# Five groups of projection columns instead of six, and one run of NSA's value products for both tiles, in a two-layer mLSTM, MoBA and NSA trunk

## The chip, the cores and the metric

The kernel runs on one core of a Trainium2 chip. The metric is the device time of one execution in microseconds; the median of the runs counts. All inputs lie in the chip's memory (HBM) when it starts, and the output is written back there. The core has TensorE (matmuls, called PE in the profile, its weight loads PEld), VectorE (DVE), ScalarE (ACT), GpSimd (POOL) and SyncE (SP, which here only issues DMAs).

## The reference

Two layers over 256 tokens of width 1024. Each layer projects the normalised input once, into 3476 columns that feed three kinds of heads, and then runs a feed-forward part:

```
for l in range(2):
    h = rmsnorm(x, norm_mix[l])
    proj = h @ w_in[l]                       # 1024 x 3476
    (m_q, m_k, m_v, m_o,                     # 512 each: mLSTM
     m_i, m_f,                               # 4 each: mLSTM's gates
     b_q, b_k, b_v,                          # 256 each: MoBA
     n_q, n_kc, n_vc,                        # 256, 64, 64: NSA, queries and compressed branch
     n_ks, n_vs, n_kw, n_vw, n_g             # 64 each and 12: NSA, selected and window branch, gates
    ) = split(proj)
    y = concat(mlstm(...), moba(...), nsa(...))
    x = x + y @ w_out[l]
    h = rmsnorm(x, norm_ffn[l])
    x = x + square(relu(h @ w_ff1[l])) @ w_ff2[l]
```

At this length MoBA is causal attention over all 256 tokens with 4 heads of 64. NSA has 4 query heads of 64 that share one key and value head per branch. Its selected branch and its window branch both become causal attention over all tokens (branches 1 and 2 in the code), its compressed branch (branch 0) attends to 15 compressed positions, and three gates per head weigh the branches.

## The kernel before, in words

The 256 tokens are two tiles of 128, `i` = 0 and 1. Every float32 product is made of three passes of a rounded type: high part times high part, high times low, low times high. Weights come from HBM in pieces into `raw` (five buffers); ACT casts a piece into its high part `hi`, DVE subtracts to get `lo` (six buffers of each). The input's parts are `H`, the mixed heads' are `Mh` and `Ml`.

The columns of the projection are cut into groups. `ORDER` (line 30) gives the order in a layer, `GROUPS` (line 378) their first column and width:

```
ORDER = ("o1", "o6", "o2", "o3", "c0", "c1", "q0", "c2", "c3", "o4", "q1", "q2", "q3", "o5")
GROUPS = {"o1": (C_NQ, 384), "o2": (C_KS, 268), "o3": (C_G, 264), "o4": (C_BK, 512), "o5": (C_MV, 512), "o6": (C_MO, 512)}
```

o1 holds NSA's queries and the inputs of its compressed branch; o2 NSA's keys and values of branches 1 and 2 and its gates; o3 mLSTM's gates and MoBA's queries; o4 MoBA's keys and values; o5 and o6 mLSTM's values and output gates. Such a group is 48 matmuls a layer in `project`: two tiles, eight blocks of 128 rows, three passes, with a block of the input as the stationary operand and the group's columns moving. Each tile's sum is one PSUM bank (tag `acc`, two of them). q0 to q3 are mLSTM's queries and keys in transposed form, c0 to c3 the weights of NSA's compression. The rest of PSUM is six banks of the tag `wk`.

The order of the work on every engine is written out by a planner (class `Flow`) while the program is built. Each part of the work is a generator that yields its operations; the planner estimates when each is ready and what it costs, and takes the next by readiness and rank. The projection, the output projection and the feed-forward part form one generator (`main`, rank 100) that fills TensorE whenever no smaller operation is ready. The casts and subtractions come up when a piece is due within a set time. A generator that asks for a buffer of a tag waits until one has been freed.

The small work that the change touches:

- `cmp_inputs` copies o1's queries into `R` (two buffers) and the compressed inputs into `KV`.
- `nsa_heads` copies o2's keys into `R`, the values into `VS`, the gates into `GT`, normalises (the power of the mean square runs on POOL, tile `hr`), rotates and transposes into `QK`.
- `gates` reads o3: mLSTM's gates into `GI`, MoBA's queries into two new `R` buffers (`R2`). `moba_heads` adds o4's keys to them, normalises and frees them.
- `score` makes the masked exponentials of NSA's scores per tile (`P`, three buffers). `attention` then runs, per tile, `attend` for branches 1 and 2: scale `P` by gate over sum, transpose it in blocks (`ident` times `P`), copy the blocks to `PT` (four buffers), and multiply with `VS` in one burst, 8 matmuls in tile 0 and 16 in tile 1, each with 64 stationary columns. The sum stays in a `wk` bank, one for each tile, until `cmp_attend` adds branch 0 (`PcT` times `VC`) and the result is split into `Mh` and `Ml`.
- `numerators` puts mLSTM's output tiles into `Y` (two buffers of 512 columns).
- `out_project` starts with NSA's and MoBA's rows and ends with mLSTM's.

Of the kernel before, what the change touches and what calls it, by code (L numbers as in the profile page):

```python
# [11 lines left out]
ALU = mybir.AluOpType  # L12
# [16 lines left out]

ORDER = ("o1", "o6", "o2", "o3", "c0", "c1", "q0", "c2", "c3", "o4", "q1", "q2", "q3", "o5")  # L30

# [251 lines left out]
def body(ctx, tc, x, w_in, b_if, conv_qk, m_norm, moba_g, nsa_qg, nsa_kg, cmp_pe, cmp_w1, cmp_w2,  # L283
# [91 lines left out]
    def rows(w, k0, kk, c0, n):  # L375
        return [(w[k0 * 128:(k0 + kk) * 128, c0:c0 + n].rearrange("(k p) n -> p k n", p=128), None)], kk, n

    GROUPS = {"o1": (C_NQ, 384), "o2": (C_KS, 268), "o3": (C_G, 264), "o4": (C_BK, 512), "o5": (C_MV, 512),
              "o6": (C_MO, 512)}
    WO_ORDER = [6, 7, 4, 5, 0, 1, 2, 3]  # L380
# [13 lines left out]
    for l in range(DEPTH):  # L394
        for name in ORDER:
            if name[0] == "c":
                s = int(name[1])
                pieces.append(([(cmp_w1[l, a, s * 512:(s + 1) * 512, :].rearrange("(k p) n -> p k n", p=128), a)
                                for a in range(2)], 8, 128))
                due.append(t)  # L400
                t += 0.45
            elif name[0] == "q":
                pieces += [rows(w_in[l], 4 * s, 4, int(name[1]) * 256, 256) for s in range(2)]
                due += [t, t + 12 * 288 / 2400]
                t += 48 * 288 / 2400
            else:
                n = GROUPS[name][1]
                pieces += [rows(w_in[l], 2 * s, 2, *GROUPS[name]) for s in range(4)]
                due += [t + 6 * s * (n + 32) / 2400 for s in range(4)]
                t += 48 * (n + 32) / 2400  # L410
# [13 lines left out]

    whole = {j for j, p in enumerate(pieces) if len(p[0]) == 2}
    raws, parts = {}, {}
# [3 lines left out]
    def loads(unsplit):  # L430

        for j, (srcs, kk, n) in enumerate(pieces):
# [8 lines left out]
            for src, a in srcs:  # L441
                dst = raw[:, :kk * n] if a is None else raw[:, a * 512:(a + 1) * 512]
                yield sy.dma_start(dst.rearrange("p (k n) -> p k n", n=n), src)
            done.add(f"raw {j}")
# [76 lines left out]
    class Layer:  # L521
        def __init__(self):
# [3 lines left out]
            for name, shape, dt in (("H", (8, 2, S), F32R), ("Mh", (8, S), F32R),  # L526
# [4 lines left out]
                setattr(self, name, keep(name, *shape, dt=dt))  # L531
            self.GT = [keep(f"GT{i}", 12) for i in range(2)]

            self.Hh, self.Hl = (self.H[:, :, a, :] for a in range(2))
            self.Fh, self.Fl = self.Hh, self.Hl

    Ls = [Layer() for _ in range(DEPTH)]
# [255 lines left out]
    def first_smalls():  # L793
        yield "H017"
        yield from small_loads(0, 0)
        yield gp.tensor_copy(B[:, 0:128], ident)
        yield gp.tensor_copy(B[:, 128:416], C[:, K_NM - 128:K_NM + 160])
        per = yield new("dg", 128)
        yield sy.dma_start(per[:64], cmp_pe.rearrange("l a (i j) d -> (l a i) (j d)", j=2))
        pps = yield wk()  # L800
        yield tr(pps[:, :64], per[:64], ident[:64, :64])
        yield dv.tensor_copy(PEs, pps[:, :64].rearrange("p (l a i) -> p l a i", l=2, a=2))
# [96 lines left out]
    def cmp_inputs(l):  # L899
# [3 lines left out]
        for i in range(2):  # L903
# [6 lines left out]
            L.R.append((yield new("R", 8, 64)))  # L910
            yield act(L.R[i][:, 0:4].rearrange("p a d -> p (a d)"), o[:, 0:256], AF.Copy, scale=L.rs[i])
            free(o)
            done.add(f"R{l}{i}")
# [20 lines left out]
    def nsa_heads(l, i):  # L934
# [4 lines left out]
        o, R, GT = L.o["o2"][i], L.R[i], L.GT[i]  # L939
        kv = o[:, 0:256].rearrange("p (a b d) -> p a b d", a=2, b=2)  # L940
        yield act(R[:, 4:6], kv[:, :, 0, :], AF.Copy, scale=L.rs[i])
        yield act(L.VS[:, i], kv[:, :, 1, :], AF.Copy, scale=L.rs[i])

        yield ts(GT, o[:, 256:268], L.rs[i], 0.5, op0=ALU.mult, op1=ALU.mult)
        free(o)
        N = yield new("N", 10, 64)
# [56 lines left out]
    def gates(l):  # L1003
# [5 lines left out]
        for i in range(2):  # L1009
            yield f"o3{l}{i}"  # L1010
            yield f"rs{l}{i}"
            o = L.o["o3"][i]
            yield stt(GI[:, i], o[:, 0:8], L.rs[i], BIFs[:, l], op0=ALU.mult, op1=ALU.add)
            L.R2.append((yield new("R", 8, 64)))
            yield act(L.R2[i][:, 0:4].rearrange("p a d -> p (a d)"), o[:, 8:264], AF.Copy, scale=L.rs[i])
            free(o)
            done.add(f"bq{l}{i}")
# [103 lines left out]

    def attend(i, P, sm, gates, o, values, last):

        nk = (i + 1) * 128
        n = len(P)
        yield dv.reciprocal(sm, sm)
        T = []
        for b in range(n):
            yield tt(sm[:, b], sm[:, b], gates[b].rearrange("p (a b) -> p b a", b=2), op=ALU.mult)
# [11 lines left out]
        ops = []  # L1141
        for b in range(n):
            for s in range(i + 1):
                for p in range(2):
                    for h in range(2):
                        ops.append(mm(o[64 * h:64 * h + 64, p, :], values(b, s, 2 * p + h),
                                      T[b * (i + 1) + s][:, 2 * p + h, :], start=b + s + p == 0,
                                      stop=last and b == n - 1 and s == i, skip_group_check=True))
        yield Burst(ops)
        free(*T)  # L1150

# [105 lines left out]

    def attention(l, units):
        L = Ls[l]
        for i, brs in units:  # L1260
            yield f"s{l}{i}{brs}"
            P, sm = L.held.pop((i, brs))
            if brs != (0,):
                o = yield wk(2, 128)
            if brs == (0,):
                yield from cmp_attend(L, i, P, sm, o)
            else:
                yield from attend(i, P, sm, [L.GT[i][:, br * 4:br * 4 + 4] for br in brs], o,
                                  lambda b, s, h: L.VS[:, s, brs[b] - 1, :], False)
            if brs == (0,):  # L1270
                yield from split(L.Mh[:, 6:8, tokens(i)], L.Ml[:, 6:8, tokens(i)], o)
                free(o)
                done.add(f"nsa{l}{i}")

# [123 lines left out]
    for l in range(DEPTH):  # L1398
        gens = [after_mix(l, i, n) for i, n in tiles] + [after_ffn(l, i, n) for i, n in tiles]
        gens += [square_scales(l), scales(l), cmp_inputs(l)]  # L1400
        gens += [nsa_heads(l, i) for i in range(2)] + [cmp_keys(l), gates(l)] + [moba_heads(l, i) for i in range(2)]
        gens += [attention(l, nsa), score(l, nsa), values(l), out_gates(l)] + [numerators(l, i) for i in range(2)]
        gens += [mlstm(l)] + [conv(l, c) for c in range(4)] + [moba_attend(l), moba_scores(l)]
# [38 lines left out]
```

## Time and profile before

| | |
|---|---|
| median of 3 runs | 639.02 us (638.28 to 639.03) |
| the profiled execution | 639.09 us, span 637.3 us from first to last instruction |
| mean granted TensorE clock | 0.999 |
| PE busy | 629.8 us, 3799 matmuls |
| DVE, ACT, POOL busy | 443.3, 366.6, 30.0 us |
| read from HBM | 111.06 MB |

A matmul record is one pass of a matmul; a float32 product that is not split by hand appears as two records. A busy time adds up what ran at any moment. The records of consecutive matmuls overlap, so the time that one costs in a dense stretch is the distance from its start to the next one's start. A row of the timeline gives the start, the length, the engine, the line (that of a helper here, the same for all), the operation, the tiles written and read, the stationary and moving sizes and how many records were merged.

### The profile page before, as it was taken

The page shows a single profiled execution, that of the slowest core. Times are in us where ns is not written, and L with a number is a line of the kernel's source. Part 1 is how long each engine was busy: PE and PEld are TensorE (multiplying, and loading weights), DVE is VectorE, ACT ScalarE, POOL GpSimd, SP SyncE. Part 2 cuts the span into 40 slices and gives each one's busy share as a digit, 9 for nine tenths or more (in the row PEclk, how much of TensorE's full clock was granted, in tenths as well). Part 3 has the DMA queues.
Part 4 walks back from the last instruction along what each step waited for, and adds up shares of the span by engine and source line. Part 5 has one row for each costly group of instructions (what it writes and reads, how often), then busy time and mean ns, then how long its engine had stood idle before and what let it go on. Part 6 is the DMA issues. An engine that isn't in the chain of part 4 may idle for free.

```text
span 637.3 us, 10219 instructions
## 1 busy us (share of the span) xinstructions
PE 629.8 (99%) x3799; PEld 544.1 (85%) x3799; DVE 443.3 (70%) x823; ACT 366.6 (58%) x718; POOL 30.0 (5%) x50
## 2 busy tenths in 40 slices
PE   9999999999999999999999999999999999999997
PEld 8898898888888888888899879988888888888885
DVE  6778899678574656656594879987776565665661
ACT  7679685655464535444465886845645554545440
POOL 1010200100000000000010111001000000000000
PEclk9999999999999999999999999999999999999999
DMA  8896524349565565646456924254466556564601
GB/s 310 238 304 210 156 67 140 124 137 284 170 203 194 182 211 160 216 163 200 125 153 212 301 69 142 69 167 152 154 212 212 184 187 209 167 214 156 222 34 67
DMA packets 79378, 112.78 MB, mean 177 GB/s; under 512 B 4928, under 2 KB 61792, under 8 KB 79328
## 3 DMA queue, kind: packets, MB, share of 16 engines
q1 hardware_dynamic: 79152, 112.05, 55.5%
q8 instruction: 30, 0.49, 0.3%
q14 instruction: 20, 0.16, 0.1%
q10 hardware_dynamic: 176, 0.07, 0.0%
HBM read 111.06 MB, written 1.05 MB: 176 GB/s over the span
## 4 chain that ended last, share of the span: by engine, by line
PE 91%; DMA 3%; ACT 2%; DVE 2%; issue 1%; POOL 1%; SPq 0%; ACTq 0%; DVEq 0%; POOLq 0%
PE wk L137 57%; PE acc L137 35%; DMA raw<-in_w_in 2%; ACT hi L137 1%; DVE lo L137 1%; DMA ident<-in_cst 1%; POOL hr L137 0%; SPq L136 0%; DVE N L137 0%; ACT QK L137 0%; POOL rs L137 0%; DVE dg L137 0%; ACT R L137 0%; DVE x L137 0%; DVE hss L137 0%
## 5 line engine op out<-in xcount | busy, mean ns | idle before, releaser
L137 DVE TENSOR_TENSOR lo<-raw,hi 128x1024 fp32r<-128x1024 f32 (+4 forms) x209 | 240.4, 1167 | 123.3 <-ACT hi L137 122.6
L137 ACT CAST hi<-raw 128x1024 fp32r<-128x1024 f32 (+3 forms) x207 | 205.9, 1015 | 135.0 <-PE wk L137 111.7
L137 PE MATMUL wk<-H,hi 128*128 128x512 f32 x512 | 128.0, 391 | 0.0
L137 PEld LDWEIGHTS wk<-H,hi 128*128 128x128 f32 x512 | 93.7, 188 | 17.9
L137 PE MATMUL acc<-hi,H 128*128 128x512 f32 (+3 forms) x368 | 99.2, 351 | 0.0
L137 PE MATMUL acc<-hi,P 128*128 128x512 f32 x240 | 79.3, 391 | 0.2 <-DVE P L137 0.2
L137 PE MATMUL wk<-hi,P 128*128 128x512 f32 x240 | 78.8, 389 | 0.0
L137 PEld LDWEIGHTS wk<-H,lo 128*128 128x128 f32 x512 | 69.9, 190 | 5.0
L137 PE MATMUL wk<-H,lo 128*128 128x256 f32 x512 | 71.4, 282 | 0.0
L137 PEld LDWEIGHTS acc<-hi,H 128*128 128x128 f32 x368 | 64.0, 188 | 6.5 <-issue 0.4
L137 PE MATMUL acc<-lo,H 128*128 128x512 f32 (+3 forms) x184 | 65.3, 355 | 0.0
L137 PEld LDWEIGHTS acc<-hi,P 128*128 128x128 f32 x240 | 45.1, 188 | 9.4 <-DVE P L137 0.6
L137 PEld LDWEIGHTS wk<-hi,P 128*128 128x128 f32 x240 | 45.0, 188 | 9.4
L137 PE MATMUL acc<-H,hi 128*128 128x256 f32 x256 | 51.5, 292 | 0.0
L137 PE MATMUL acc<-lo,P 128*128 128x512 f32 x120 | 47.0, 392 | 0.0
L137 PE MATMUL wk<-lo,P 128*128 128x512 f32 x120 | 46.7, 389 | 0.0
L137 ACT COPY th<-wk 128x256 f32<-128x256 f32 x64 | 23.9, 373 | 35.7 <-PE wk L137 35.7
L137 PEld LDWEIGHTS acc<-H,hi 128*128 128x128 f32 x256 | 40.7, 190 | 0.5 <-ACT hi L137 0.2
L137 PEld LDWEIGHTS acc<-lo,H 128*128 128x128 f32 x184 | 34.6, 188 | 3.4 <-issue 0.3
L137 PE MATMUL acc<-H,lo 128*128 128x256 f32 x128 | 36.7, 287 | 0.0
L137 ACT ACTIVATE H<-wk,V 128x128 fp32r<-128x128 f32 x64 | 18.1, 375 | 21.1 <-PE wk L137 21.1
L137 ACT CAST P<-cv 128x512 fp32r<-128x512 f32 x30 | 18.6, 621 | 17.3 <-DVE cv L137 17.3
(199 smaller groups left out, 799.5 us busy)
## 6 DMA issues: line engine op xcount, KB each, us to landing
raw<-in_w_ff SPq DMA_DIRECT2D x128, 512.0 KB, 4.4
raw<-in_w_in SPq DMA_DIRECT2D x40, 512.0 KB, 5.0
raw<-in_w_out SPq DMA_DIRECT2D x16, 512.0 KB, 4.0
whole<-in_cmp_w SPq DMA_DIRECT2D x16, 256.0 KB, 5.0
raw<-in_w_in SPq DMA_DIRECT2D x8, 384.0 KB, 3.9
raw<-in_w_in SPq DMA_DIRECT2D x8, 268.0 KB, 3.5
raw<-in_w_in SPq DMA_DIRECT2D x8, 264.0 KB, 3.2
out<-x SPq DMA_DIRECT2D x4, 256.0 KB, 2.0
```

Of the source, the lines that this page charges most:

```text
L137: o = Op(self.name, lambda: f(out, *args, **kw), outs, ins, self.cost(op, outs, ins))
```

## The change

It does four things. The three groups o1, o2 and o3 become two: o1 takes the KS columns behind its own (448 columns), and o2 takes the rest of the old o2 and all of the old o3 (468 columns, loaded by two DMAs to a piece). A bank of o2 is freed when both of its readers, `nsa_heads` and `gates`, have read it. MoBA's queries (`R2`) go into the two `Y` buffers instead of `R`. NSA's `attention` becomes `nsa_attend`: the weights of both tiles are scaled and transposed first, those of tile 0 into the two `Y` buffers and those of tile 1 into `PT`; then all 24 value products run as one burst into one `wk` bank, and then the compressed branch is added for both tiles. Besides, the small load of `cmp_pe` goes into a `Y` buffer and is issued ahead of the other small loads.

```diff
-ORDER = ("o1", "o6", "o2", "o3", "c0", "c1", "q0", "c2", "c3", "o4", "q1", "q2", "q3", "o5")
+ORDER = ("o1", "o6", "o2", "c0", "c1", "q0", "c2", "c3", "o4", "q1", "q2", "q3", "o5")
...
-    GROUPS = {"o1": (C_NQ, 384), "o2": (C_KS, 268), "o3": (C_G, 264), "o4": (C_BK, 512), "o5": (C_MV, 512),
-              "o6": (C_MO, 512)}
+    GROUPS = {"o1": (C_NQ, 448), "o2": (C_KS + 64, 468), "o4": (C_BK, 512), "o5": (C_MV, 512), "o6": (C_MO, 512)}
...
-                pieces += [rows(w_in[l], 2 * s, 2, *GROUPS[name]) for s in range(4)]
+                if name == "o2":
+                    pieces += [([(w_in[l, 256 * s:256 * s + 256, c0:c0 + m].rearrange("(k p) n -> p k n", p=128),
+                                      slice(at, at + m)) for c0, m, at in ((C_KS + 64, 204, 0), (C_G, 264, 204))], 2, n)
+                                   for s in range(4)]
+                else:
+                    pieces += [rows(w_in[l], 2 * s, 2, *GROUPS[name]) for s in range(4)]
...
+            self.left = [2, 2]
+        def read(self, i):
+            self.left[i] -= 1
+            if not self.left[i]:
+                free(self.o["o2"][i])
...
         yield "H017"
+        per = yield new("Y", 512)
+        yield sy.dma_start(per[:64, :128], cmp_pe.rearrange("l a (i j) d -> (l a i) (j d)", j=2))
         yield from small_loads(0, 0)
...
-        per = yield new("dg", 128)
-        yield sy.dma_start(per[:64], cmp_pe.rearrange("l a (i j) d -> (l a i) (j d)", j=2))
...
+            yield act(L.R[i][:, 4], o[:, 384:448], AF.Copy, scale=L.rs[i])
             free(o)
...
-        yield act(R[:, 4:6], kv[:, :, 0, :], AF.Copy, scale=L.rs[i])
-        yield act(L.VS[:, i], kv[:, :, 1, :], AF.Copy, scale=L.rs[i])
-        yield ts(GT, o[:, 256:268], L.rs[i], 0.5, op0=ALU.mult, op1=ALU.mult)
-        free(o)
+        yield act(R[:, 5], o[:, 64:128], AF.Copy, scale=L.rs[i])
+        yield act(L.VS[:, i], o[:, 0:256].rearrange("p (a b) -> p a b", a=2)[:, :, 0:64], AF.Copy, scale=L.rs[i])
+        yield ts(GT, o[:, 192:204], L.rs[i], 0.5, op0=ALU.mult, op1=ALU.mult)
+        L.read(i)
...
-            o = L.o["o3"][i]
-            yield stt(GI[:, i], o[:, 0:8], L.rs[i], BIFs[:, l], op0=ALU.mult, op1=ALU.add)
-            L.R2.append((yield new("R", 8, 64)))
-            yield act(L.R2[i][:, 0:4].rearrange("p a d -> p (a d)"), o[:, 8:264], AF.Copy, scale=L.rs[i])
-            free(o)
+            o = L.o["o2"][i]
+            yield stt(GI[:, i], o[:, 204:212], L.rs[i], BIFs[:, l], op0=ALU.mult, op1=ALU.add)
+            L.R2.append((yield new("Y", 8, 64)))
+            yield act(L.R2[i][:, 0:4].rearrange("p a d -> p (a d)"), o[:, 212:468], AF.Copy, scale=L.rs[i])
+            L.read(i)
...
-                T.append((yield new("PT", 4, 128)))
-                yield copy(T[-1], pt)
+                T.append((b, s, (yield new("PT" if i else "Y", 4, 128))))
+                yield copy(T[-1][2], pt)
...
+    def nsa_attend(l, brs):
+        L = Ls[l]
+        T = []
+        for i in range(2):
+            yield f"s{l}{i}{brs}"
+            P, sm = L.held.pop((i, brs))
+            T.append((yield from weighted(i, P, sm, [L.GT[i][:, br * 4:br * 4 + 4] for br in brs])))
+        o = yield wk(2, 2, 128)
+        yield Burst([mm(o[64 * h:64 * h + 64, i, p, :], L.VS[:, s, brs[b] - 1, :], t[:, 2 * p + h, :],
+                        start=i + b + s + p == 0, stop=False, skip_group_check=True)
+                     for i in range(2) for b, s, t in T[i] for p in range(2) for h in range(2)])
+        free(*(t for u in T for *_, t in u))
+        for i in range(2):
+            yield f"s{l}{i}{(0,)}"
+            yield from cmp_attend(L, i, *L.held.pop((i, (0,))), o[:, i])
+            yield from split(L.Mh[:, 6:8, tokens(i)], L.Ml[:, 6:8, tokens(i)], o[:, i])
+            done.add(f"nsa{l}{i}")
+        free(o)
```

More of the change, by code (lines that the diff above doesn't have):

```diff
@@ L423, in body @@
                 t += 12 * 544 / 2400
-    whole = {j for j, p in enumerate(pieces) if len(p[0]) == 2}
+    whole = {j for j, p in enumerate(pieces) if p[1] == 8}
     raws, parts = {}, {}
@@ L441, in loads @@
             for src, a in srcs:
-                dst = raw[:, :kk * n] if a is None else raw[:, a * 512:(a + 1) * 512]
-                yield sy.dma_start(dst.rearrange("p (k n) -> p k n", n=n), src)
+                dst = raw[:, a * 512:(a + 1) * 512] if j in whole else raw[:, :kk * n]
+                dst = dst.rearrange("p (k n) -> p k n", n=n)
+                yield sy.dma_start(dst[:, :, a] if isinstance(a, slice) else dst, src)
             done.add(f"raw {j}")
@@ L797, in first_smalls @@
         yield gp.tensor_copy(B[:, 128:416], C[:, K_NM - 128:K_NM + 160])
-        per = yield new("dg", 128)
-        yield sy.dma_start(per[:64], cmp_pe.rearrange("l a (i j) d -> (l a i) (j d)", j=2))
         pps = yield wk()
-        yield tr(pps[:, :64], per[:64], ident[:64, :64])
+        yield tr(pps[:, :64], per[:64, :128], ident[:64, :64])
         yield dv.tensor_copy(PEs, pps[:, :64].rearrange("p (l a i) -> p l a i", l=2, a=2))
@@ L939, in nsa_heads @@
         o, R, GT = L.o["o2"][i], L.R[i], L.GT[i]
-        kv = o[:, 0:256].rearrange("p (a b d) -> p a b d", a=2, b=2)
-        yield act(R[:, 4:6], kv[:, :, 0, :], AF.Copy, scale=L.rs[i])
-        yield act(L.VS[:, i], kv[:, :, 1, :], AF.Copy, scale=L.rs[i])
-        yield ts(GT, o[:, 256:268], L.rs[i], 0.5, op0=ALU.mult, op1=ALU.mult)
-        free(o)
+        yield act(R[:, 5], o[:, 64:128], AF.Copy, scale=L.rs[i])
+        yield act(L.VS[:, i], o[:, 0:256].rearrange("p (a b) -> p a b", a=2)[:, :, 0:64], AF.Copy, scale=L.rs[i])
+        yield ts(GT, o[:, 192:204], L.rs[i], 0.5, op0=ALU.mult, op1=ALU.mult)
+        L.read(i)
         N = yield new("N", 10, 64)
@@ L1009, in gates @@
         for i in range(2):
-            yield f"o3{l}{i}"
+            yield f"o2{l}{i}"
             yield f"rs{l}{i}"
-            o = L.o["o3"][i]
-            yield stt(GI[:, i], o[:, 0:8], L.rs[i], BIFs[:, l], op0=ALU.mult, op1=ALU.add)
-            L.R2.append((yield new("R", 8, 64)))
-            yield act(L.R2[i][:, 0:4].rearrange("p a d -> p (a d)"), o[:, 8:264], AF.Copy, scale=L.rs[i])
-            free(o)
+            o = L.o["o2"][i]
[3 more added lines that the diff above has]
+            L.read(i)
             done.add(f"bq{l}{i}")
@@ L1120, in scores, with weighted @@
         return P, sm
-    def attend(i, P, sm, gates, o, values, last):
+    def weighted(i, P, sm, gates):
         nk = (i + 1) * 128
-        n = len(P)
         yield dv.reciprocal(sm, sm)
         T = []
-        for b in range(n):
-            yield tt(sm[:, b], sm[:, b], gates[b].rearrange("p (a b) -> p b a", b=2), op=ALU.mult)
+        for b, gate in enumerate(gates):
+            yield tt(sm[:, b], sm[:, b], gate.rearrange("p (a b) -> p b a", b=2), op=ALU.mult)
             for p in range(2):
@@ L1136, in attend @@
                 yield Burst([tr(pt[:, h, :], P[b][:, h, s * 128:(s + 1) * 128], ident) for h in range(4)])
-                T.append((yield new("PT", 4, 128)))
-                yield copy(T[-1], pt)
+                T.append((b, s, (yield new("PT" if i else "Y", 4, 128))))
+                yield copy(T[-1][2], pt)
                 free(pt)
             free(P[b])
[L1141 to L1150, printed above, removed]
+        return T
     def moba_scores(l):
@@ L1256, in score @@
             done.add(f"s{l}{i}{brs}")
-    def attention(l, units):
+    def nsa_attend(l, brs):
         L = Ls[l]
-        for i, brs in units:
+        T = []
+        for i in range(2):
             yield f"s{l}{i}{brs}"
             P, sm = L.held.pop((i, brs))
[L1263 to L1273, printed above, removed]
+            T.append((yield from weighted(i, P, sm, [L.GT[i][:, br * 4:br * 4 + 4] for br in brs])))
[10 more added lines that the diff above has]
+        free(o)
     def values(l):
@@ L1401, in body @@
         gens += [nsa_heads(l, i) for i in range(2)] + [cmp_keys(l), gates(l)] + [moba_heads(l, i) for i in range(2)]
-        gens += [attention(l, nsa), score(l, nsa), values(l), out_gates(l)] + [numerators(l, i) for i in range(2)]
+        gens += [nsa_attend(l, (1, 2)), score(l, nsa), values(l), out_gates(l)] + [numerators(l, i) for i in range(2)]
         gens += [mlstm(l)] + [conv(l, c) for c in range(4)] + [moba_attend(l), moba_scores(l)]
```

## The prediction

> **What bounds the kernel now.** I read the page first (busy times, the chain that ended last), then the busy time by stage, then the matmuls in order of time. From the page:
>
> ```profile
> PE 629.8 (99%) x3799; PEld 544.1 (85%) x3799; DVE 443.3 (70%) x823; ACT 366.6 (58%) x718; POOL 30.0 (5%) x50
> ...
> PEclk9999999999999999999999999999999999999999
> ...
> PE 91%; DMA 3%; ACT 2%; DVE 2%; issue 1%; POOL 1%; SPq 0%; ACTq 0%; DVEq 0%; POOLq 0%
> ```
>
> TensorE is busy for 629.8 of 637.3 us at full clock, and 91% of the chain is its own. The program is one queue of matmuls that hardly ever waits, so a change is worth what it takes out of that queue, and costs what makes the queue wait. By stage of the first layer (columns: window, length, then busy us of PE, PEld, DVE, ACT, POOL, clock, DMA share, GB/s):
>
> ```profile
> 0.00:6.50 6.50, 5.29 (x53) 4.94 (x53) 1.58 (x8) 2.23 (x5) 0.80 (x8) 1.00 0.67 195
> 6.50:16.80 10.30, 10.30 (x63) 9.71 (x62) 9.13 (x25) 10.11 (x25) 1.35 (x3) 1.00 1.03 379
> ...
> 29.10:40.50 11.40, 11.40 (x96) 11.40 (x95) 5.76 (x19) 6.95 (x14) 2.05 (x2) 1.00 1.01 327
> 40.50:53.00 12.50, 12.29 (x159) 11.16 (x157) 12.07 (x33) 12.17 (x32) 1.06 (x4) 1.00 0.95 300
> 53.00:69.00 16.00, 16.00 (x96) 12.23 (x93) 13.41 (x37) 14.34 (x39) 2.73 (x3) 1.00 0.49 144
> 69.00:98.00 29.00, 29.00 (x273) 27.46 (x272) 26.67 (x70) 21.77 (x67) 2.03 (x5) 1.00 0.30 93
> 98.00:115.00 17.00, 17.00 (x106) 14.41 (x105) 14.84 (x28) 9.27 (x20) 0.00 (x0) 1.00 0.48 155
> ```
>
> The window from 29.1 to 40.5 is o2 and o3, the two groups that the change merges. There VectorE is half idle; from 40.5 to 115 it is nearly full, and this will be a rival below.
>
> **The change part by part.**
>
> *Three groups become two.* o1, o2 and o3 (384, 268 and 264 columns) become o1 and o2 (448 and 468). The columns are 916 both times; each group has 48 matmuls in a layer (2 tiles, 8 blocks of rows, 3 passes), so 48 go in each layer, 96 in all. A busy PE row's mean duration overlaps the next matmul, so I take the pace from starts: every third matmul is the one with the low part.
>
> ```profile
> 12.02 0.33 PE L137 MATMUL acc<-lo,H 128*128 128x384 f32 x1
> ...
> 14.62 0.37 PE L137 MATMUL acc<-lo,H 128*128 128x384 f32 x1
> ...
> 18.67 0.39 PE L137 MATMUL wk<-lo,H 128*128 128x512 f32 x1
> ...
> 22.09 0.39 PE L137 MATMUL wk<-lo,H 128*128 128x512 f32 x1
> ...
> 29.47 0.29 PE L137 MATMUL acc<-lo,H 128*128 128x268 f32 x1
> ...
> 34.55 0.29 PE L137 MATMUL acc<-lo,H 128*128 128x268 f32 x1
> ...
> 35.28 0.28 PE L137 MATMUL acc<-lo,H 128*128 128x264 f32 x1
> ...
> 39.66 0.28 PE L137 MATMUL acc<-lo,H 128*128 128x264 f32 x1
> ```
>
> Between these rows lie 15, 15, 42 and 36 matmuls: 0.1733 us each at 384 columns, 0.2280 at 512, 0.1210 at 268, 0.1217 at 264. One matmul of each old group takes 0.1733 + 0.1210 + 0.1217 = 0.4160 us. No row has 448 or 468 columns. On the line between 384 and 512 they take 0.2007 and 0.2092, together 0.4099. The saving is 0.0061 x 96 = 0.6 us. The ends: if both ran at the price of 512, 0.4560 against 0.4160 is a loss of 3.8 us; if both ran at the price of 384, a gain of 6.7 us. Both need a step inside a range where the rows rise evenly, so for the range I use a narrower pair, the gain of 0.6 and the 0.3 of the second rival.
>
> The Trainium skill, "TensorE: Matmul & The Clock Gate", section "Back-to-back issue gap", prices a warm matmul at its columns by 2.4 GHz plus 2.5 ns. By it the 96 matmuls would be worth 0.24 us, an estimate from that page, and the total would fall by 0.4 us less. The trace does not agree on the level: the page gives 215.8 ns at 512 columns, where the rows above give 228.0.
>
> *The value products of both tiles in one run.* Each tile's products are matmuls with 64 stationary columns, in pairs that run side by side (16 records are 8 pairs). They interrupt the projection twice a layer; the change leaves one interruption with the same 24 pairs. What the first one costs beyond its pairs:
>
> ```profile
> 63.93 0.55 PE L137 MATMUL wk<-CW,KV 128*128 128x64 f32 x4
> 64.29 0.48 PE L137 MATMUL acc<-hi,H 128*128 128x512 f32 x1
> 64.70 1.09 PE L137 MATMUL wk<-PT,VS 128*64 128x128 f32 x16
> 65.72 0.50 PE L137 MATMUL acc<-lo,H 128*128 128x512 f32 x1
> 66.06 0.40 PE L137 MATMUL acc<-hi,H 128*128 128x512 f32 x1
> ...
> 95.39 1.97 PE L137 MATMUL wk<-PT,VS 128*64 128x128 f32 x32
> 97.28 0.39 PE L137 MATMUL acc<-H,hi 128*128 128x256 f32 x1
> ...
> 376.31 0.40 PE L137 MATMUL acc<-lo,H 128*128 128x512 f32 x1
> 376.63 1.09 PE L137 MATMUL wk<-PT,VS 128*64 128x128 f32 x16
> 377.66 0.66 PE L137 MATMUL wk<-CW,KV 128*128 128x64 f32 x4
> 378.13 0.71 PE L137 MATMUL acc<-hi,H 128*128 128x512 f32 x2
> ```
>
> Sixteen pairs take 97.28 - 95.39 = 1.89 us and eight take 65.72 - 64.70 = 1.02, so a pair costs 0.109 and a run 0.15 beside its pairs. Going in at 376.31 costs 0.32 less the matmul's 0.23: 0.09. Coming back at 65.72 costs 0.34 less 0.23: 0.11. In layer 0 that is 0.35 us for the run that goes. In layer 1 the CW products follow directly and take 0.47 to the next projection matmul where they took 0.36 alone at 63.93, so there it is 0.09 + 0.15 + 0.11, again 0.35. Two layers: 0.7 us. Upper end 0.9 (the whole 0.41 - 0.23 before the run at 64.70 counted); lower end 0.3, if one layer's shorter run had found company anyway.
>
> *A larger first group.* o1's first piece grows by 64 columns of 256 rows, 66 kB. At the 195 and 379 GB/s of the first two windows it lands 0.34 or 0.17 us later; I take 0.25, and the loads of x queued behind it on SP's queue land later by as much. On VectorE the start is a chain:
>
> ```profile
> 5.35 0.62 DVE L137 CAST hi<-raw 128x384 fp32r<-128x384 f32 x2
> 5.88 1.02 DVE L137 TENSOR_TENSOR lo<-raw,hi 128x384 fp32r<-128x384 f32 x2
> 6.82 2.15 DVE L137 SCALAR_TENSOR_TENSOR H<-wk,V,H 128x128 fp32r<-128x128 f32 x8
> ...
> 9.35 0.51 PE L137 MATMUL acc<-hi,H 128*128 128x384 f32 x2
> ...
> 9.89 0.44 PE L137 MATMUL acc<-lo,H 128*128 128x384 f32 x1
> ```
>
> The 1.47 us from 5.35 to 6.82 grow by up to a sixth, 0.25. So the first products come 0.25 to 0.5 us later. Some comes back: before 9.89 TensorE waited for the second piece's low part (0.54 less two matmuls' 0.35, 0.19 us), and twelve longer matmuls in front fill that. I take +0.2 us, ends 0.05 and 0.5.
>
> *Edits that I cost at nothing.* The extra copy of the KS columns with o1, four fewer casts and four fewer subtractions a layer lie beside the projection on ACT and VectorE, with the pieces prepared ahead. The new o2 has two DMAs to a piece, eight issues a layer, as o2 and o3 had together; SP's queue is no longer. The load of cmp_pe moves ahead of the small constants, half a microsecond of SP's queue. If this cover went, the price is a late piece, at most one subtraction (about a microsecond) a layer. The o2 banks now serve two readers: the first is needed again only when q0 starts, a half group and the compress products later.
>
> *The added waits.* MoBA's scaled queries and the first NSA tile's transposed weights share the two Y buffers. So the first NSA tile's copies into Y, on ACT, stand behind MoBA's normalisation of o4, whose power runs on POOL, and casts of the next pieces are queued behind them on ACT. The order is planned with that in mind; it goes wrong when POOL is late. The trace has one such case, in layer 1:
>
> ```profile
> 356.35 0.28 PE L137 MATMUL acc<-H,lo 128*128 128x256 f32 x1
> 357.29 0.44 PE L137 MATMUL wk<-ident,N 128*128 128x128 f32 x2 [0.66 <-DVE N L137]
> ...
> 348.23 1.33 POOL L137 TENSOR_TENSOR hr<-hss,negh 128x6 f32<-128x6 f32 x1 [20.29 <-DVE hss L137]
> 353.22 2.62 POOL L137 TENSOR_TENSOR hr<-hss,negh 128x6 f32<-128x6 f32 x1 [3.66 <-DVE hss L137]
> ```
>
> The second power took 2.62 us instead of 1.33, and TensorE stood 0.94 - 0.12 = 0.8 us before the transposes. All of this moves in the changed kernel, because tile 1 of o2 ends with the whole merged group. The stall may go (0.8 gained) or another may come; I count nothing for it and keep 0.8 to each side.
>
> *The sum.* The profiled execution took 639.09 us (span 637.3, 1.8 around it), 0.07 above the median of 639.02. 639.09 - 0.6 - 0.7 + 0.2 = 638.0; against the median 637.9. That is 1.1 us or 0.17%, just under the 0.2% (1.3 us) that a measurement of this kernel can tell from no change.
>
> **The rivals.**
>
> *The stall goes as well.* With 0.8 us more the time is 637.1. For it: of the two powers shown only one was late, and both move. Against: they run again, in places as crowded. Chance 0.25.
>
> *A matmul's fixed part is smaller than the local line says.* Through the rows of 268 and 512 columns the slope is 0.1070 / 244 = 0.000439 us a column and the fixed part 0.2280 - 512 x 0.000439 = 0.0032 us; 96 of those are 0.3 us. The time is then 638.2, inside the bound. Against: 384 lies 1.6 ns above that line. The Trainium skill's page named above comes near this case. Chance 0.2.
>
> *VectorE falls behind and the output projection waits.* This is the case on the other side. Tile 0 of o2 now ends about 3 us later, tile 1 about 6 us later, so at most some 3 us of VectorE's NSA work (about half of that window's 5.76, an estimate) move past 40.5, where its idle time is 0.4 + 2.6 + 2.3 + 2.2 = 7.5 us up to 115. The output projection needs NSA and MoBA then:
>
> ```profile
> 109.23 1.53 PE L137 MATMUL wk<-PT,VB 128*64 128x128 f32 x24
> ...
> 115.74 0.48 PE L137 MATMUL acc<-hi,Mh 128*128 128x512 f32 x1
> ```
>
> MoBA's products are queued at 109.2, their first use comes 12 matmuls after 115.7, at 118.4, so some 7 us are spare. It decides only if the delay passes those 7 us; each microsecond beyond costs one in each layer. A delay of 9 gives 4 us, 642. Against it: 3 us of moved work, 7.5 us of room. Chance 0.1.
>
> **How the numbers follow.** The forecast, 637.9, has 0.45, with its own range 637.2 to 638.6 from the ends of the first three terms; the stall that goes has 0.25, the small fixed part 0.2, the late VectorE 0.1. Faster by over 0.2% means below 637.74: 0.17 of the forecast's 0.45, all of the 0.25, and 0.03 of the 0.2, together 0.45. Slower by over 0.2% means above 640.3: most of the slow rival, 0.09. The rest, 0.46, is within the bound. The range for 8 in 10 goes from 636.7 (stall gone, upper ends) to 639.2 (small fixed part and one new stall of 0.8).
>
> **What would show it.** PE's records should be fewer by 96, with starts 0.20 and 0.21 us apart at 448 and 468 columns; one PT,VS run of 48 records a layer, 24 x 0.109 + 0.15 = 2.8 us long; the first projection matmul near 6.7 instead of 6.48; the output projection of layer 0 starting about 0.5 us earlier than 115.74. I am wrong if the 468-column matmuls start more than 0.22 us apart, if TensorE's idle time before N transposes or ACT's copies into PT or Y grows past a microsecond, or if the first output-projection matmul of a layer waits for Mh.

## The result: slower by 1.1%, and the profile after

The changed kernel takes 645.8 us (median of 4 runs, 645.05 to 647.38) where the kernel before took 638.65 on the same chip (637.47 to 639.03): a ratio of 1.0109, 95% interval 1.0094 to 1.0125. The forecast was 637.9 in a range of 636.7 to 639.2, so it was wrong in sign, and the median lies 6.6 us above the range. The profiled execution took 645.05 us (span 643.3). The versions further down were each measured beside the kernel before on the same chip, where that one took 639.4 to 639.9 us: compare their ratios rather than their times.

From the page of the changed kernel: busy times, granted clock in 40 slices, shares of the chain that ended last.

```profile
PE 631.7 (98%) x3700; PEld 541.4 (84%) x3700; DVE 444.2 (69%) x815; ACT 369.0 (57%) x714; POOL 32.2 (5%) x50
...
PEclk9989999999999999999999999999999999999999
...
PE 81%; issue 5%; DMA 4%; DVE 4%; ACT 2%; POOL 2%; SPq 1%; ACTq 0%; POOLq 0%; DVEq 0%
```

TensorE has 99 records fewer (96 were meant), and yet is busy longer: one slice near the start has a lower clock. Its share of the chain fell from 91% to 81%, but that alone does not point at the loss: a version further down that is faster than the kernel before (o2 of 472 columns) has 81% too. The loads show more. The list of waits of SP's queue has this line (us in total, times, longest), where the kernel before had one such wait of 1.0 us:

```profile
SPq L136 <- DMA raw<-in_w_in: 23.3, 12, 3.2
```

A DMA to `raw` now waits for another DMA to `raw`. Eight of the twelve waits, 19.5 us of the 23.3, are those of the second DMAs of o2's pieces, four in each layer. The timeline of SP's queue in layer 0 shows which:

```profile
17.67 11.43 SPq L136 DMA_DIRECT2D raw<-in_w_in  x7
...
30.12 0.43 SPq L136 DMA_DIRECT2D th<-in_sel  x1
31.56 0.38 SPq L136 DMA_DIRECT2D raw<-in_w_in  x1
```

Seven of the eight DMAs of o2's pieces take 11.43 us to issue, the eighth follows at 31.56. In the program the second DMA of a piece (264 columns) waits for the first one (204 columns) of the same `raw` buffer to land. The columns do not overlap, but within a partition the two DMAs write interleaved stretches of one buffer, and in this build they are ordered one behind the other. By issue and landing in the trace the first parts are issued at 17.67, 21.77, 25.31 and 28.67 and land at 21.23, 24.83, 28.19 and 31.55; the second parts are issued at 21.30, 24.85, 28.21 and 31.56, and land at 24.25, 27.65, 30.98 and 35.52. SP's queue goes out in order, so everything behind stands too: `th<-in_sel` is issued at 30.12, in the kernel before at 23.90. While it stands, the DMA engines have little to do. Stages of the changed kernel (columns as before: window, length, PE, PEld, DVE, ACT, POOL, granted clock, DMA share, GB/s):

```profile
20.00:25.00 5.00, 5.00 (x25) 3.75 (x24) 3.67 (x6) 2.85 (x7) 2.43 (x2) 1.00 0.43 124
25.00:30.00 5.00, 5.00 (x24) 4.10 (x23) 3.47 (x6) 1.87 (x3) 0.00 (x0) 1.00 0.45 121
33.60:36.90 3.30, 0.81 (x4) 0.20 (x2) 1.20 (x2) 2.46 (x3) 0.00 (x0) 1.00 1.08 324
36.90:40.90 4.00, 4.00 (x12) 3.44 (x13) 1.04 (x2) 1.15 (x2) 0.00 (x0) 0.60 1.11 354
```

and of the kernel before:

```profile
20.00:25.00 5.00, 5.00 (x25) 3.88 (x25) 3.63 (x9) 2.04 (x4) 0.00 (x0) 1.00 0.92 256
25.00:30.00 5.00, 5.00 (x28) 4.26 (x27) 2.95 (x7) 3.21 (x6) 0.00 (x0) 1.00 0.82 239
```

From 20 to 30 us the DMA share falls from 0.92 and 0.82 to 0.43 and 0.45. TensorE feels nothing of it there (5.00 of 5.00): it works on pieces that are in already. Then it runs dry. The chain that ended last, in order of time, for the changed kernel:

```profile
25.31 2.88 DMA raw<-in_w_in
28.21 0.37 SPq L136
...
30.12 4.04 DMA th<-in_sel
...
34.70 0.98 ACT hi L137
```

`sel`, a constant of 256 kB queued behind three of the four waits, lands at 34.16. ACT's next instruction needs it, and the cast of o2's third piece, which has been in since 30.98, stands behind that one on ACT; the cast of the fourth piece, in at 35.52, follows:

```profile
34.18 0.62 ACT L137 CAST SEL<-th 128x512 fp32r<-128x512 f32 x1 [4.87 <-DMA th<-in_sel]
34.70 1.94 ACT L137 CAST hi<-raw 128x936 fp32r<-128x936 f32 x2
```

TensorE's timeline:

```profile
33.54 0.38 PE L137 MATMUL acc<-hi,H 128*128 128x468 f32 x1
35.72 0.48 PE L137 MATMUL acc<-hi,H 128*128 128x468 f32 x1 [1.81 <-ACT hi L137]
36.89 0.49 PE L137 MATMUL acc<-lo,H 128*128 128x468 f32 x1 [0.69 <-DVE lo L137]
...
37.95 0.98 PE L137 MATMUL acc<-hi,H 128*128 128x468 f32 x2
...
41.07 0.41 PE L137 MATMUL acc<-lo,H 128*128 128x468 f32 x1
```

From 33.54 to 36.89 only two matmuls start: 3.35 us less two at 0.213, 2.9 us lost. From 37.95 to 41.07 eight matmuls take 0.39 us each instead of 0.213: the clock of 0.60 in the window from 36.9, another 1.4 us. Later in layer 0 the same interruptions of the projection are longer than in layer 1:

```profile
50.45 0.28 PE L137 MATMUL acc<-H,hi 128*128 128x256 f32 x1
...
52.64 0.36 PE L137 MATMUL acc<-H,hi 128*128 128x256 f32 x1
...
55.20 0.28 PE L137 MATMUL acc<-H,lo 128*128 128x256 f32 x1
...
61.29 0.48 PE L137 MATMUL acc<-hi,H 128*128 128x512 f32 x1
...
365.50 0.28 PE L137 MATMUL acc<-H,hi 128*128 128x256 f32 x1
...
365.98 0.36 PE L137 MATMUL acc<-H,hi 128*128 128x256 f32 x1
...
368.55 0.28 PE L137 MATMUL acc<-H,lo 128*128 128x256 f32 x1
...
373.12 0.47 PE L137 MATMUL acc<-hi,H 128*128 128x512 f32 x1
```

The first takes 2.19 us against 0.48 (1.7 lost, mostly behind ACT's KV), the second 6.09 against 4.57 (1.5 lost, behind the weights of c2 and c3 among others). Together 2.9 + 1.4 + 1.7 + 1.5 = 7.5 us, all in layer 0. Layer 1 has the same four waits, but its pieces are loaded further ahead and TensorE does not stall for them. The stages by TensorE's starts, for the profiled executions (us; the projection runs from its first matmul to the first one of the output projection):

| kernel | projection, layer 0 | projection, layer 1 | last matmul |
|---|---|---|---|
| before / before, profiled again | 109.3 / 109.9 | 109.2 / 109.6 | 632.3 / 633.3 |
| after | 116.9 | 107.8 | 638.6 |
| o2 of 472 columns, no wait | 110.4 | 107.8 | 631.1 |
| the same, value products in two runs | 110.2 | 108.0 | 631.6 |
| DMAs in pairs of pieces | 112.8 | 107.8 | 634.1 |
| second DMA on GpSimd | 113.8 | 108.4 | 635.7 |
| four DMAs to a piece, 468 / 472 columns | 115.1 / 116.8 | 107.8 / 107.8 | 636.4 / 637.6 |
| before, with such waits | 115.9 | 108.3 | 639.0 |
| before, with the merged run alone | 109.5 | 108.2 | 631.9 |

### The profile page after: what moved, and what is told of

The parts are those of the page before. It is cut to its first block, busy times and chain, and to the rows that moved or that the text cites. A ratio compares the mean times of both kernels' runs of the same rounds, so it can differ in the third digit from the quotient of the medians.

```text
span 643.3 us, 10014 instructions
## 1 busy us (share of the span) xinstructions
PE 631.7 (98%) x3700; PEld 541.4 (84%) x3700; DVE 444.2 (69%) x815; ACT 369.0 (57%) x714; POOL 32.2 (5%) x50
## 4 chain that ended last, share of the span: by engine, by line
PE 81%; issue 5%; DMA 4%; DVE 4%; ACT 2%; POOL 2%; SPq 1%; ACTq 0%; POOLq 0%; DVEq 0%
PE wk L137 52%; PE acc L137 29%; DMA raw<-in_w_in 2%; POOL hr L137 1%; DMA whole<-in_cmp_w 1%; DVE lo L137 1%; SPq L136 1%; ACT P L137 1%; DMA th<-in_sel 1%; DMA ident<-in_cst 1%; ACT hi L137 0%; DVE N L137 0%; ACT H L137 0%; POOL rs L137 0%; DVE P L137 0%
## 5 line engine op out<-in xcount | busy, mean ns | idle before, releaser
L137 DVE TENSOR_TENSOR lo<-raw,hi 128x1024 fp32r<-128x1024 f32 (+3 forms) x201 | 239.5, 1207 | 133.0 <-ACT hi L137 131.9
L137 ACT CAST hi<-raw 128x1024 fp32r<-128x1024 f32 (+2 forms) x199 | 204.3, 1049 | 130.9 <-PE wk L137 112.1
L137 PE MATMUL acc<-hi,H 128*128 128x512 f32 (+2 forms) x304 | 98.2, 395 | 1.8 <-ACT hi L137 1.8
L137 PEld LDWEIGHTS acc<-hi,H 128*128 128x128 f32 x304 | 57.1, 191 | 10.7 <-ACT hi L137 2.2
L137 PE MATMUL acc<-lo,H 128*128 128x512 f32 (+2 forms) x152 | 59.9, 394 | 0.9 <-DVE lo L137 0.9
L137 PE MATMUL acc<-H,hi 128*128 128x256 f32 x256 | 49.1, 287 | 0.0
L137 PEld LDWEIGHTS acc<-lo,H 128*128 128x128 f32 x152 | 29.0, 191 | 5.8 <-DVE lo L137 1.3
L137 DVE TENSOR_TENSOR cx<-wk,th 128x256 f32<-128x256 f32 x64 | 27.0, 421 | 2.2 <-ACT th L137 2.2
```

The source lines that it names most:

```text
L137: o = Op(self.name, lambda: f(out, *args, **kw), outs, ins, self.cost(op, outs, ins))
```

## The experiments

The theory: the second DMA of an o2 piece waits in SP's queue for the first, the DMA engines stand idle, and layer 0 pays. The rivals: the narrow DMAs are slow in themselves; the new order of the work on ACT, VectorE and TensorE stalls with or without them; the merged run of value products is at fault.

**The wait taken away: o2 of 472 columns.** With a first part of 208 columns, four of them unused KS columns, the program has no such wait.

```diff
-    GROUPS = {"o1": (C_NQ, 448), "o2": (C_KS + 64, 468), "o4": (C_BK, 512), "o5": (C_MV, 512), "o6": (C_MO, 512)}
+    GROUPS = {"o1": (C_NQ, 448), "o2": (C_KS + 60, 472), "o4": (C_BK, 512), "o5": (C_MV, 512), "o6": (C_MO, 512)}
...
-                                      slice(at, at + m)) for c0, m, at in ((C_KS + 64, 204, 0), (C_G, 264, 204))], 2, n)
+                                      slice(at, at + m)) for c0, m, at in ((C_KS + 60, 208, 0), (C_G, 264, 208))], 2, n)
...
```

The rest of the edit moves the readers' columns by four.

> The changed kernel, with four more columns (the last of KS) at the front of o2: its first part is 208 columns wide instead of 204, and the second DMA of a piece no longer waits for the first. Theory W (the wait of the second DMA holds SP's queue, and all that is lost is lost in layer 0 behind it): the stall near 33 us, the half clock behind it and the two stalls at 50 and 55 us go, some 8 us; 0.2 us come on top for 96 matmuls of four more columns; 637 to 638.5 us, level with or just under the kernel before. Rival R (the merged group ends late, VectorE and ACT fall behind whatever the DMAs do): 644 to 646 as the changed kernel. Rival H (half is the wait, half the bunching of the small work): 640 to 643.

Measured: 638.59 us, ratio 0.9977 (0.9965 to 0.9989). The program has the same number of instructions, and TensorE's records are the same in the same order. SP's queue waits for DMAs to `raw` 3.0 us in all, and the DMA engines are full:

```profile
SPq L136 <- DMA raw<-in_w_in: 3.0, 10, 0.6
```

```profile
20.00:25.00 5.00, 5.00 (x26) 3.70 (x24) 3.45 (x7) 2.74 (x5) 0.00 (x0) 1.00 1.04 328
25.00:30.00 5.00, 5.00 (x24) 4.14 (x23) 3.59 (x7) 3.75 (x5) 0.00 (x0) 1.00 1.05 325
```

So 1.3% hangs on four columns of a load, by way of the wait that they decide, and the rest of the change makes the kernel 0.23% faster. The new order of the work and the merged run are both in this version, so neither of them carries the loss. Layer 0 still has a microsecond of the loss:

```profile
48.24 0.28 PE L137 MATMUL acc<-H,lo 128*128 128x256 f32 x1
...
53.83 0.48 PE L137 MATMUL acc<-hi,H 128*128 128x512 f32 x1
```

This is the interruption that took 4.57 us in layer 1 above, here 5.59. Less that 1.0, the 7.5 us are 6.5, and the table's layer 0 has 116.9 - 110.4 = 6.5. Why the program has a wait at 204 columns and none at 208 stays open. When it is built with other widths, a first part of 204, 206, 210, 212, 220, 228 or 236 columns brings the wait and one of 208, 216, 224, 232, 240 or 248, all multiples of 8, does not; of these only 204 and 208 were run.

**Half the waits.** The same DMAs and waits, but the first parts of two pieces are issued ahead of their second parts; TensorE's order is all but the changed kernel's.

```diff
+        held = []
...
-                yield sy.dma_start(dst[:, :, a] if isinstance(a, slice) else dst, src)
-            done.add(f"raw {j}")
+                if isinstance(a, slice) and a.start:
+                    held.append((j, dst[:, :, a], src))
+                else:
+                    yield sy.dma_start(dst[:, :, a] if isinstance(a, slice) else dst, src)
+            if len(held) == 2:
+                for i, d, s in held:
+                    yield sy.dma_start(d, s)
+                    done.add(f"raw {i}")
+                held = []
+            elif not held:
+                done.add(f"raw {j}")
```

> The changed kernel with the DMAs of o2's pieces issued in pairs of pieces: first parts of two pieces, then their second parts. Every second part still waits for its own first part, with the same DMAs of 816 and 1056 B rows; the waits of two pieces now run at the same time, so SP's queue is held some two times 3 us a layer instead of four. TensorE's order is all but that of the changed kernel. If the loss is the DMA engines standing still while the queue is held (DMA share 0.43 and 0.45 from 20 to 30 us in the changed kernel, 1.04 and 1.05 where nothing waits, some 6 us of loading lost): the share comes to 0.65 to 0.8 in that window, half of the loss comes back, and the time is 641 to 643 (ratio 1.002 to 1.006). If the narrow DMAs themselves are what is slow, or the four waits cost only through what stands behind the last: 644 to 646 (1.007 to 1.011).

Measured: 641.36 us, ratio 1.0035 (1.0019 to 1.005).

```profile
SPq L136 <- DMA raw<-in_w_in: 10.1, 8, 3.7
```

```profile
20.00:25.00 5.00, 5.00 (x24) 3.76 (x23) 3.21 (x6) 1.84 (x5) 0.34 (x1) 1.00 0.63 192
25.00:30.00 5.00, 5.00 (x24) 4.07 (x24) 3.38 (x6) 3.02 (x4) 0.00 (x0) 1.00 0.92 252
```

Waits of 23.3, 10.1 and 3.0 us give ratios of 1.0109, 1.0035 and 0.9977, and the DMA share rises as the waits shrink. The narrow DMAs are the same here as in the changed kernel, and all but four columns the same in the one without the wait, so they are not slow in themselves.

**The wait put into the kernel before.** Its o2 pieces loaded by two DMAs that overlap by two columns, so that the second waits.

```diff
-                pieces += [rows(w_in[l], 2 * s, 2, *GROUPS[name]) for s in range(4)]
+                if name == "o2":
+                    g0 = GROUPS[name][0]
+                    pieces += [([(w_in[l, 256 * s:256 * s + 256, g0 + at:g0 + to].rearrange("(k p) n -> p k n", p=128),
+                                  slice(at, to)) for at, to in ((0, 136), (134, n))], 2, n) for s in range(4)]
+                else:
+                    pieces += [rows(w_in[l], 2 * s, 2, *GROUPS[name]) for s in range(4)]
...
```

> The kernel before with o2's pieces (268 columns) loaded by two DMAs whose columns overlap by two, so that each second DMA waits for the first to land: four such waits a layer, nothing else changed. Theory W: SP's queue is held for some 3 us four times in layer 0 as in the changed kernel, and the pieces behind come late: 4 to 9 us slower than the kernel before; layer 1 hardly touched. Rival R: no change beyond 0.5 us, since the wait was hidden.

Measured: 645.97 us, ratio 1.0098 (1.008 to 1.0117). The loss comes without five groups and without the merged run, in TensorE's old order. (Its DMAs are narrower as well, 544 and 536 B a row, which this run does not tell apart from the waits.) It comes at another place, though:

```profile
24.31 0.25 PE L137 MATMUL wk<-ident,dg 96*128 96x96 f32 x1
29.46 0.36 PE L137 MATMUL wk<-ident,dg 64*128 64x64 f32 x1 [4.90 <-DMA dg<-in_cmp_pe]
```

Here `cmp_pe` stands in the held queue, and its transpose stands first in TensorE's. The clock is 0.50 from 26.5 to 33.3. What is queued behind a held load sets where it hurts.

**The second DMA on GpSimd.** TensorE's order is exactly that of the changed kernel.

```diff
-                yield sy.dma_start(dst[:, :, a] if isinstance(a, slice) else dst, src)
+                yield (gp if isinstance(a, slice) and a.start else sy).dma_start(dst[:, :, a] if isinstance(a, slice) else dst, src)
```

> The changed kernel with one edit: the second DMA of each o2 piece (264 columns) is issued by GpSimd instead of SyncE; TensorE's order of instructions is the same as in the changed kernel, and the second DMA still waits for the first one. Theory A, what costs is that the waits hold everything behind them in SP's queue: SP's waits for DMA raw fall from 23.3 us to under 5, TensorE's stall of 3.3 us at 33.6 and the 12 matmuls at half clock behind it go, sel lands before 30, and the time is 638.5 to 640 (ratio 0.998 to 1.001). Theory B, what costs is that the second parts themselves land late, from whichever queue: the waits of 3 us stand on POOL's queue, TensorE stalls as before for the low part of o2's third and fourth piece, and the time stays at 644 to 646 (ratio 1.008 to 1.010). Between them, if POOL's own copies of B behind the waits come late for MoBA's scores: 641 to 643.

Measured: 643.52 us, ratio 1.0049 (1.0031 to 1.0067): between the two theories. SP is free, but GpSimd waits and the second parts land late all the same (27.67 to 33.86, by landing):

```profile
22.26 2.32 POOL L136 DMA_DIRECT2D raw<-in_w_in  x3 [5.75 <-DMA raw<-in_w_in]
```

```profile
31.76 0.48 PE L137 MATMUL acc<-lo,H 128*128 128x468 f32 x1 [0.50 <-DVE lo L137]
...
34.08 0.48 PE L137 MATMUL acc<-lo,H 128*128 128x468 f32 x1 [0.78 <-DVE lo L137]
```

Four short waits of this kind, 1.7 us in all, take the place of the long one, and no slice of that page has a clock below 9 tenths. So what is queued behind the waits on SP is worth about half of the loss, the late pieces and the rest about the other half. The split is rough: the first of the second parts lands later than in the changed kernel (27.67 against 24.25), and layer 1 has a wait of 0.8 us that the changed kernel does not have.

**Four DMAs to a piece**, 128 rows each, without waits, eight more issues a layer: first with 468 columns, then with 472.

```diff
-                    pieces += [([(w_in[l, 256 * s:256 * s + 256, c0:c0 + m].rearrange("(k p) n -> p k n", p=128),
-                                      slice(at, at + m)) for c0, m, at in ((C_KS + 64, 204, 0), (C_G, 264, 204))], 2, n)
-                                   for s in range(4)]
+                    pieces += [([(w_in[l, 256 * s + 128 * k:256 * s + 128 * k + 128, c0:c0 + m], (k, slice(at, at + m)))
+                                 for k in range(2) for c0, m, at in ((C_KS + 64, 204, 0), (C_G, 264, 204))], 2, n)
+                               for s in range(4)]
...
```

> The changed kernel with o2's pieces loaded by four DMAs, each into one unbroken stretch: no wait, exactly 468 columns, but 8 more issues a layer on SP's queue, some 3 us of its time each layer. Theory W: 637 to 638.5 us, within 0.5 of the kernel with 208 columns; SP's issue time is hidden. Rival R: 644 to 646. If it is issue time on SP's queue and not the wait that hurts, this is slower than the changed kernel.

> The version with o2 of 472 columns, first part 208, each piece loaded by four DMAs of 128 rows instead of two of 256: eight more issues a layer on SP's queue, no waits. The kernel with 468 columns and four DMAs took 642.8 (ratio 1.0046) where two unhindered DMAs took 638.6. If the eight issues cost (8 times about 0.5 us of SP's queue, in the stretch from 17 to 30 us in which everything else is loaded): 642 to 643 (1.004 to 1.006), with late weights of the compress products and TensorE waits of over 2 us between 40 and 57. If that loss came from how the order of that one kernel happened to fall, with a late POOL power: 638.3 to 640 (0.997 to 1.001).

Measured: 642.8 us, ratio 1.0046 (1.0031 to 1.006), and 644.17, ratio 1.0064 (1.0041 to 1.0088). The first fits none of the cases that were expected, the second lies just above the case in which the issues cost. Without the wait the kernel still loses, then. In the 472-column form the loads are slower than with two DMAs:

```profile
20.00:25.00 5.00, 5.00 (x25) 3.75 (x24) 3.87 (x7) 3.31 (x6) 0.24 (x1) 1.00 0.91 273
25.00:30.00 5.00, 5.00 (x24) 4.10 (x23) 2.60 (x6) 2.46 (x4) 0.00 (x0) 1.00 0.79 210
```

SP issues one such DMA about every 0.47 us (25.92, 26.39, 26.86, 27.34), of 121 kB on average: 256 GB/s, below the 325 that the same columns reach in half as many DMAs. An issue takes longer than the 0.37 us in which 121 kB would move at 325 GB/s (worked out from these two numbers). The Trainium skill ("DMA: Bandwidth & Descriptors", section "Issuing engines are not separate DMA queues") calls the time to initiate a DMA usually small beside the DMA itself. Beside the 3.30 us from issue to landing of the DMA at 25.92 it is small here too; beside the 0.37 us it is not.

That this rate is the cause of the loss is not shown. The order of work differs too, and TensorE waits for `N` and `KV` three times between 48.0 and 52.0 us (1.08, 0.83 and 1.08). The first of these follows a slow power on POOL, 2.37 us (from 45.30) where it takes 1.34 in the 472-column kernel with two DMAs. And then the clock is 0.50 for 6.8 us, in the 468-column form (the second line) as well:

```profile
52.30:59.10 6.80, 6.68 (x54) 5.13 (x54) 4.55 (x18) 5.29 (x11) 0.00 (x0) 0.50 0.65 213
50.80:57.50 6.70, 6.12 (x48) 4.76 (x47) 5.85 (x24) 5.97 (x12) 0.93 (x4) 0.50 0.92 294
```

Half of 6.8 is up to 3.4 us, an estimate; with the 3.0 us of waits that is about what layer 0 loses against the version with two DMAs (116.8 against 110.4). How much of it follows from the issues stays open.

**The small loads later.** The changed kernel with `sel` and the others started a tile later.

```diff
-        yield "o100"
+        yield "o201"
```

> The changed kernel with the second lot of small loads (sel, CW, MN and others) and the work on them started when tile 1 of o1's successor group o2 has begun its end (the mark o201) instead of at the end of o1's first tile (o100); the waiting pairs of DMAs stay. If ACT's wait of 4.87 us for sel, with the cast of o2's last piece queued behind it, is a main part of the stall: TensorE's stall near 33.6 shrinks from 3.3 us to under 1.5, no half clock behind it, and the time is 641 to 643 (ratio 1.003 to 1.007). If the held queue alone decides, through the late last piece and late c0 and c1 weights: 645 (1.009 to 1.011), with the four waits of some 3 us in SP's queue as long as before in both cases.

Measured: 650.85 us, ratio 1.0179 (1.0147 to 1.0211): slower still, outside both expectations. The wait for `sel` went, and TensorE's wait of 1.81 us for the third piece's cast with it (one of 0.93 for the fourth piece's cast stands there now), but the cast of a q0 piece came to stand on ACT ahead of the copy that frees o6's bank. First TensorE, then ACT:

```profile
42.16 0.76 PE L137 MATMUL acc<-hi,H 128*128 128x468 f32 x1 [3.95 <-ACT g L137]
```

```profile
40.47 1.04 ACT L137 CAST hi<-raw 128x1024 fp32r<-128x1024 f32 x1 [4.82 <-DMA raw<-in_w_in]
```

Twice after such stalls the clock is 0.50 for 6.8 us here (from 40.1 and from 53.8). How much `sel` alone is worth in time is not settled by it. That another instruction was next in line to wait for the late loads, it shows.

**The other parts of the change.** The merged run alone, on the kernel before:

```diff
...
-        gens += [attention(l, nsa), score(l, nsa), values(l), out_gates(l)] + [numerators(l, i) for i in range(2)]
+        gens += [nsa_attend(l, (1, 2)), score(l, nsa), values(l), out_gates(l)] + [numerators(l, i) for i in range(2)]
```

> The kernel before with the single run of NSA's value products alone; six groups, loads as before. By the prediction's working 0.35 us a layer go: 0.7 us under the kernel before, ratio 0.9989. If merging the run is what bunches the small work and stalls TensorE, it is slower by some us.

Measured: 639.24 us, ratio 0.9992 (0.9981 to 1.0004). And the five groups alone, the 472-column kernel with the reverse of that diff:

> The version of the changed kernel in which no DMA waits (o2 of 472 columns, first part 208), with NSA's value products of the two tiles in two runs as before, so that only the five groups are left of the change. If the merged run is worth the 0.5 us that it gave alone: 639.1 by the scale of the 208 version's 638.6 (ratio to before 0.9985, 0.998 to 0.9995). If the merged run gave nothing there: 638.6 (0.9975). If the groups themselves give nothing and the 208 version's gain was the merged run and the absent stall of 0.8 us: 639.7 (1.000).

Measured: 638.31 us, ratio 0.9974 (0.9959 to 0.9988), against 0.9977 with the merged run. So the gain comes with the five groups and what belongs to them (the load of `cmp_pe`, MoBA's queries in `Y`), and the merged run's share cannot be told from nothing, nor from the 0.7 us forecast. The kernel before, profiled again:

> The kernel before, profiled once more, for the stall of 0.8 us before the transposes of N at 357.29 in layer 1. If it belongs to the order of that kernel, POOL's second power of the layer again takes about 2.6 us and TensorE again waits 0.7 us or more for N; then part of what the version with 208 columns gained is that stall. If it was one execution's accident, the power takes 1.3 us, the wait is under 0.2, and the projection of layer 1 takes about 108.3 us instead of 109.2.

Measured: 640.1 us for this one run, and the stall in layer 1 is there again; first its second power in layer 1, then that of the kernel with the merged run alone:

```profile
354.21 2.62 POOL L137 TENSOR_TENSOR hr<-hss,negh 128x6 f32<-128x6 f32 x1 [4.12 <-DVE hss L137]
```

```profile
353.76 1.38 POOL L137 TENSOR_TENSOR hr<-hss,negh 128x6 f32<-128x6 f32 x1 [3.63 <-DVE hss L137]
```

The same operation with the same subtraction running beside it on VectorE takes 2.62 us in both profiles of the kernel before and 1.37 or 1.38 in the others. The stall of 0.8 us belonged to that kernel, and it is gone in the changed one. It does not come from TensorE's order: the kernel before with waits has the same order there, and its power takes 1.38 us. Why the power is slow stays open.

The best version is that with 472 columns, with the merged run or without: 0.23% or 0.26% under the kernel before.

## Why the prediction was wrong, point by point

**The step that failed: "Edits that I cost at nothing".** That paragraph said that the new o2 has eight issues a layer as o2 and o3 had together, that "SP's queue is no longer", and that a lost cover costs a late piece and at most a microsecond a layer. The count was right. That the two DMAs write one buffer, and that the second could be ordered behind the first, was not asked. The queue was longer by those waits, 9.2 us in layer 0; the DMA share fell to about half for ten microseconds, and layer 0 lost 7.5 us. The price was too low as well: a late piece does not cost one subtraction once the loads are what everything waits for, since ACT, VectorE and TensorE each had an instruction next in line that needed them, and the stall of some 3 us brought a slower clock on top, 1.4 us more. In the window of DMA shares the warning stood: 1.03 from 6.5 to 16.8 and 1.01 from 29.1 to 40.5 left little room in the loads of layer 0 (0.80 between them), and the prediction read these rows only for the rate and for the other engines.

**Pace, -0.6: it is 0.** The prediction took 448 and 468 columns to lie on a line between 384 and 512. In the changed kernel, layer 1:

```profile
330.85 0.37 PE L137 MATMUL acc<-lo,H 128*128 128x448 f32 x1
...
335.11 0.36 PE L137 MATMUL acc<-lo,H 128*128 128x448 f32 x1
...
351.04 0.38 PE L137 MATMUL acc<-lo,H 128*128 128x468 f32 x1
...
360.63 0.38 PE L137 MATMUL acc<-lo,H 128*128 128x468 f32 x1
```

21 matmuls in 4.26 us are 0.2029 each, 45 in 9.59 are 0.2131: together 0.4160, exactly the 0.4160 of the three old groups, where 0.4099 was forecast. The rival with the small fixed part (0.3) was nearer, and still too high.

**The merged run, -0.7.** Its length was right, 2.8 us forecast, 2.78 here:

```profile
100.42 1.09 PE L137 MATMUL wk<-Y,VS 128*64 128x128 f32 x16
...
103.20 0.33 PE L137 MATMUL wk<-ident,Pc 128*128 128x128 f32 x1
```

What it saves is not resolved: 0.5 us alone (between 1.2 gained and 0.3 lost by the interval) and about nothing beside the five groups. Both are within the error of nothing and of the 0.7.

**The start, +0.2.** The first projection matmul came at 7.05, forecast 6.7. But it came at 6.48 and 6.71 in two profiles of the same kernel before, and at 6.07 in the 472-column one, so this term is smaller than what one profile can show.

**The stall in layer 1, counted 0: it went, 0.8 us.** The rival that said so had the mechanism right. Without the held loads the change gains some 1.5 us (0.23%, with an interval of 0.11 to 0.35%), so the forecast of 1.1 comes near its size, but by luck: out of a pace that is 0, a run whose saving is not resolved and a stall counted at 0. In the changed kernel this gain stands in the table's layer 1, 107.8 instead of 109.2. The two versions with six groups that do not have the stall take 108.2 and 108.3 there, so most of it is the stall.

**VectorE falling behind**, the slow rival, was not seen: the first output-projection matmul of layer 0 came 8 us late because of the loads, and layer 1 had no wait before it.

## What to carry to other kernels

A load that is split in two has to be looked at as two writes into one buffer: see in the waits of the queue whether the second is issued before the first has landed. A wait in an in-order queue costs what stands behind it, so read what comes next there, and the DMA share of that stage: in layer 0, where it was 0.92 to 1.11 after the stretch that the waits emptied, the time that the DMA engines stood idle was not made up; in layer 1, with pieces loaded further ahead, the same waits cost nothing. More DMAs without a wait were no remedy here, though why is only in part known.

## What the runs showed of the hardware

The half clock came after short stalls. In the changed kernel 3.35 us with two matmuls in them were enough (clock 0.60 from 36.9 to 40.9, back by 41.07). The 4.9 us in the kernel before with waits led to it too (clock 0.50 from 26.5 to 33.3, TensorE at work again from 29.46), and so did the three waits of 1.08, 0.83 and 1.08 us, within 4.0 us, in the kernel with four DMAs and 472 columns. The Trainium skill ("TensorE: Matmul & The Clock Gate", section "What's actually happening") states half rate after an idle window of about 3.4 us and full rate after about as much work. The traces agree roughly on the length of the stall, except that the windows here were not quite empty. On the way back the first two agree, but the one with four DMAs does not: the clock stayed at 0.50 for 6.8 us with TensorE busy for 6.68 of them. No threshold can be read from this: two stalls of 0.5 and 0.8 us, 2 us apart, left the clock alone, and so did two of 0.87 and 1.85 us between 45.8 and 49.0 in the kernel with DMAs in pairs.
